# Attention two query tiles a step, tiles at multiples of 512 bytes, first transfers by need, and a spread output border in a fused attention and recurrence layer

## The chip, the cores and the metric

The kernel runs on one core of one Trainium2 chip. The time is device microseconds of one execution of the whole program. TensorE is PE, VectorE is DVE, ScalarE is ACT, GpSimd is POOL and SyncE is SP; PEld is PE's loading of stationary operands.

## The reference

One layer on x, 512 tokens by 2048 features in fp32: normalization, one input projection, an attention group and a recurrence group side by side, one output projection and the residual.

```python
h = rms_norm(x, norm_w)
q, k, v, g_attn, xr, g_lru = split(h @ w_in)     # 1024 | 256 | 256 | 1024 | 1024 | 1024 columns
attn_out = attention_group(q, k, v, ...)          # 8 heads of 128, 2 key/value heads, RMS norm and RoPE on q, k
lru_out = lru_group(xr, ...)                      # 4-tap convolution, then a gated linear scan forward and one backward
mixed = concat([rms_norm(attn_out, attn_norm_w) * silu(g_attn),
                rms_norm(lru_out, lru_norm_w) * silu(g_lru)])
return x + mixed @ w_out                          # w_out is 2048 x 2048
```

## The kernel before, in words

**Products.** Every fp32 operand is split into two tiles, `hi` (rounded, by an ACT cast) and `lo` (the rest, by a DVE subtraction); `wsplit` (L199 to L207) does so for the weights. `mm3` (L145 to L148) issues three matmuls per product: hi·hi, hi·lo, lo·hi. A matmul streams 512 columns of the moving operand past a stationary tile of 128x128, and PE loads the next stationary tile while the present one's columns stream.

**Memory.** Pools are stacked in the on-chip memory from two sides. On the left lie constants, raw weights (`wr`), split weights and the turned x (`xw`), later the outputs stage's residual tiles and part of its operands (`out`). On the right lies first a tile `end` of 24 floats a partition (L100), then the rings of hidden tiles (`hq`), the recurrence (`lru`), keys and values (`qkv`), a second pool of split weights (`wx`, which `wsplit` uses every other time while it is open), attention (`att`) and the final stage (`fin`). So the size of `end` decides at which address, modulo 512 bytes, all tiles on the right begin. PSUM has eight banks: four of tag `pj`, taken by `pj()` mostly for projections, and four of tag `mm`, taken in a ring by `mm()` for scores, transposes and values.

**Start.** `xload` fetches x in chunks of 256 features (the first in two halves), `wraw` fetches raw weights (the first in two halves on ACT's queue), and `columns` (L176 to L182) turns the norm's gain vector `nw_st` on PE, so that x's evacuation can scale by it. `xturn` (L227 to L234) turns x by four PE transposes a tile and evacuates it on ACT and DVE. Until then `busy` issues small warm-up matmuls (L935): WARM of them in front, WARM2 behind the first transposes.

**Stages.** The projection of the recurrence's input (`proj_feat`, L283) runs to about 40 us of the trace, the two halves of the recurrence with the other projection as filler to about 220, K, V and Q to about 285 (`proj_tok`, L321), attention to about 441, the attention's gate projection to 495, and the outputs to 650.

**Attention.** `weave` (L324) alternates a chain and a filler: each `yield n` of `attention` (L608) lets the gates' projections advance by n yields, each six matmuls on a `pj` bank. One step is one query tile of one head: `weights` (L567) makes scores (three matmuls on an `mm` bank), takes the row maximum on DVE (L574), exponentiates on ACT (L577) and scales on POOL (L579); two steps later `turn_weights` (L582) turns the weights by four transposes on an `mm` bank (L586), with a cast on ACT (L588) and a subtraction on DVE (L589); after four tiles `values` (L591) makes the head's output on an `mm` bank and copies it out on DVE (L600). `turned` (L561, through `turn`, L534) turns the queries of a later head by four transposes. Within a step the order is scores, (turned queries), (values), turned weights. The gates' sigmoid products (`gate`, L634 to L645) run on ACT and DVE among these.

**Outputs.** The last product is made from seven block products a level instead of eight, in two passes over P1, Q6, Q5, Q7 and P2, Q3, Q4 (`PASS`, L797). `uses` (L799) lists them in order; `prepare` (L814) splits raw or summed weight blocks into a ring of seven operand tiles, of which entries 0 to 2 lie in `fin` on the right and 3 to 6 in `out` on the left. The left operands, eight mixed tiles made by `seven` (L693), lie on the right for numbers 0 to 4 and in `out` for 5 to 7. The matmuls are L902; `done` (L858) adds each product into the residual tiles on DVE and stores them. `last_gates` (L1095), advanced by `outputs` once at each P1 use, makes the last three left operands. ACT's, DVE's and SP's instructions there stand in the order in which the program writes them.

Of the kernel before, what the change touches and what calls it, by code (L numbers as in the profile page):

```python
# [11 lines left out]
F32 = mybir.dt.float32  # L12
# [5 lines left out]
P = 128  # L18
# [5 lines left out]
NH = 8  # L24
# [16 lines left out]
WARM, WARM2 = 13, 6  # L41


STEPS = 2
# [12 lines left out]
def hybrid_kernel(  # L57
# [42 lines left out]
    opened("end", "right").tile([P, 24], F32, tag="end", name="end")  # L100
# [87 lines left out]
    def wraw(w, r0, c0, nk=1, queue=nc.sync):  # L188

        raw = pools["wr"].tile([P, 2, SEQ], F32, tag="wr", bufs=3, name=nm("wr"))  # L190
        src = w[r0 : r0 + 2 * P, c0 : c0 + SEQ].rearrange("(k p) e -> p k e", p=P)
        for k in range(nk):
# [6 lines left out]
    def wsplit(raw, k):  # L199

        turn_of[0] += k
        pool = pools["wx" if "wx" in pools and turn_of[0] % 2 else "xw"]
        hi = pool.tile([P, SEQ], F32R, tag="wh", bufs=4, name=nm("wh"))
        lo = pool.tile([P, SEQ], F32R, tag="wl", bufs=4, name=nm("wl"))
        nc.scalar.copy(hi, raw[:, k, :])  # L205
        nc.vector.tensor_sub(lo, raw[:, k, :], f(hi))  # L206
        return hi, lo  # L207
# [10 lines left out]
    def xload(c, nk=1):  # L218

        xc = b4(shape=(P, NT, 2 * P))  # L220
        for k in range(nk):
            ks = slice(k * 2 * P // nk, (k + 1) * 2 * P // nk)
            cs = slice(c * 2 * P + ks.start, c * 2 * P + ks.stop)
            nc.sync.dma_start(xc[:, :, ks], xf[:, cs].rearrange("(t p) d -> p t d", p=P))
            yield xc
# [341 lines left out]
    def weights(q, g, t):  # L567

        qh, ql = q
        tt = slice(t * P, (t + 1) * P)  # L570
        sc = mm()
        mm3(sc, qh[:, tt], ql[:, tt], kth[g], ktl[g], True, True)
        mx = pools["att"].tile([P, 1], F32, tag="mx", bufs=6, name=nm("mx"))
        nc.vector.tensor_reduce(mx, sc, axis=AX.X, op=ALU.max, negate=True)  # L574
        p = k2()
        sm = pools["att"].tile([P, 1], F32, tag="sm", bufs=6, name=nm("sm"))
# [31 lines left out]
    def attention(rots):  # L608

        qs, ps_, pts = {h: turned(rots[0], h) for h in range(2)}, {}, {}  # L610
        yield 13
        last = NH * NT
        for i in range(last + 3):
            h, t = divmod(i, NT)
            if i < last:
                ps_[i] = weights(qs[h], h // G, t)
                if t == 0 and h + 2 < NH:
                    qs[h + 2] = turned(rots[(h + 2) // G], (h + 2) % G)
            j = i - 3
            if j >= 0 and j % NT == NT - 1:  # L620
                values(j // NT, *pts.pop(j // NT))
            j = i - 2
            if 0 <= j < last:
                h, t = divmod(j, NT)
                if t == 0:
# [67 lines left out]
    def seven(src, op, hi, lo):  # L693

        src = halves(src)
        res = combine(src, op)
        for to, part in ((slice(0, 3), src[:, 1:4]), (slice(3, 7), res)):
            nc.scalar.copy(hi[:, to], part)
            nc.vector.tensor_sub(lo[:, to], part, f(hi[:, to]))

# [96 lines left out]
    TAIL = 2  # L797
# [43 lines left out]
    def outputs(work):  # L841

        bank, tmp, at = {}, {}, [0]
# [13 lines left out]
        def done(g, name, s):  # L857
# [14 lines left out]
            elif name == "Q7":  # L872
# [3 lines left out]
                v.tensor_add(b10, b10, tmp["c", s])  # L876
# [32 lines left out]
        for n, use in enumerate(order_):  # L909
# [6 lines left out]
            if g == 0 and not second and k == 0:  # L916
                next(work, None)
# [28 lines left out]
    with tc.high_priority():  # L946
        xs, ws = xload(0, 2), wraw(w_in, 0, C_XR, 2, nc.scalar)
        xc, raw = next(xs), next(ws)
        nc.scalar.dma_start(nw_st, norm_w.rearrange("(k p) -> k p", p=P))
# [4 lines left out]
        first = [wsplit(raw, 0)]  # L954
# [103 lines left out]
    def build(i, pair, where):  # L1058
        mixed[i][1] = hi, lo = where(7)
        seven(pair, ALU.subtract, hi, lo)  # L1060

    for q in range(4):
        for _ in range(2):
            next(fill, None)
        build(q, hp[q], lambda n: kept(pools["fin"]))
# [3 lines left out]
    def later():  # L1069
# [6 lines left out]
        build(4, ap_[0], lambda n: [hring.tile([P, n, H], F32R, name=nm(t)) for t in ("mh", "ml")])  # L1076
# [18 lines left out]
    def last_gates():  # L1095
        yield
        build(5, ap_[1], lambda n: last_mixed[0])
        yield
        todo = gate(gs, ap_[2:], R_AN + 4, fin_s)
        for _ in range(3):  # L1100
            next(todo)
        yield
        build(6, ap_[2], lambda n: last_mixed[1])
        drain(todo)
        yield
        build(7, ap_[3], lambda n: last_mixed[2])
        yield
# [48 lines left out]
```

## Time and profile before

| quantity | value |
|---|---|
| median of three runs (lowest, highest) | 658.29 us (656.95, 658.40) |
| the profiled execution's own time | 657.07 us |
| its span, first to last instruction | 655.3 us |
| PE busy | 647.8 us in 2960 instructions |
| DVE, ACT, POOL busy | 485.8, 344.4, 96.5 us |
| granted TensorE clock | full in every slice |
| PE waits in the view of waits | three, of 1.5, 1.1 and 0.5 us |

Views of the profile: the page sums up each engine; the view of waits says for which tile an engine waited, written by whom and at which line; the chain of waits follows the work that ended last back in time; windows and the timeline show a stretch. A row as `L588 ACT CAST pt<-mm` is line 588 on ACT, writing tile `pt` from tile `mm`; what stands in brackets is the idle time before it and what ended it. A matmul's listed duration overlaps its neighbours, so what PE pays is the distance from one start to the next.

### The profile page before, as it was taken

Reading aid. Unit: us, or ns where it says so; the run is one execution under the profiler, and the core shown is the slowest. Engines: PE = TensorE matmul, PEld = TensorE weight load, DVE = VectorE, ACT = ScalarE, POOL = GpSimd, SP = SyncE. Lnnn points to the kernel's source line nnn. Section 1 sums busy time; section 2 is a strip of 40 time slices with the busy share of each in tenths; the row PEclk is TensorE's granted clock in tenths of the full one; section 3 lists DMA queues with packets and bytes.
Section 4 is the critical chain, followed back from the end, with each engine's and each line's share of the span. In section 5 each row is a group of like instructions: output and inputs, shape, how many; then the busy total and the mean of one; then the engine's idle time right before and its main releaser. Section 6 shows DMA issues by size and latency. Waiting matters only on the chain.

```text
span 655.3 us, 8600 instructions
## 1 busy us (share of the span) xinstructions
PE 647.8 (99%) x2960; PEld 532.1 (81%) x2960; DVE 485.8 (74%) x832; ACT 344.4 (53%) x639; POOL 96.5 (15%) x127
## 2 busy tenths in 40 slices
PE   8999999999999999999999999999999999999997
PEld 6888888888888888888888888888888878888875
DVE  5778679977687925855955568439948997698994
ACT  3543799489856515454735456335434564344441
POOL 0000000000022312132543435411000000100000
PEclk9999999999999999999999999999999999999999
DMA  9933253322334331446776678663355667585322
GB/s 292 312 107 113 65 139 95 98 65 65 97 114 129 95 98 33 122 141 147 170 177 149 196 150 193 151 144 111 96 191 197 256 208 248 179 297 177 131 78 96
DMA packets 53067, 96.96 MB, mean 148 GB/s; under 512 B 4316, under 2 KB 14688, under 8 KB 52896
## 3 DMA queue, kind: packets, MB, share of 16 engines
q1 hardware_dynamic: 45648, 75.17, 36.2%
q0 software_dynamic: 7056, 20.72, 13.6%
q10 hardware_dynamic: 320, 0.53, 0.3%
q8 instruction: 23, 0.38, 0.2%
q14 instruction: 20, 0.16, 0.1%
HBM read 92.21 MB, written 20.98 MB: 173 GB/s over the span
## 4 chain that ended last, share of the span: by engine, by line
PE 96%; DVE 1%; DMA 1%; issue 1%; ACT 0%; ACTq 0%; DVEq 0%
PE pj L146 20%; PE pj L148 20%; PE pj L147 20%; PE mm L902 12%; PE pj L902 9%; PE mm L146 3%; PE mm L148 3%; PE mm L147 3%; PE mm L586 2%; PE mm L231 1%; PE pj L292 1%; PE mm L534 1%; DMA nw_st<-in_norm_w_dram 1%; DVE ol L717 0%; DMA rw<-in_w_out_dram 0%
## 5 line engine op out<-in xcount | busy, mean ns | idle before, releaser
L146 PE MATMUL pj<-x,wh 128*128 128x512 f32 x376 | 150.5, 400 | 0.0
L148 PE MATMUL pj<-x,wl 128*128 128x512 f32 x376 | 146.8, 390 | 0.0
L147 PE MATMUL pj<-x,wh 128*128 128x512 f32 x376 | 146.6, 390 | 0.0
L205 ACT CAST wh<-wr 128x512 fp32r<-128x512 f32 x144 | 86.1, 618 | 70.4 <-PE pj L148 26.2
L206 DVE TENSOR_TENSOR wl<-wr,wh 128x512 fp32r<-128x512 f32 x144 | 98.7, 706 | 29.7 <-ACT wh L205 29.7
L148 PEld LDWEIGHTS pj<-x,wl 128*128 128x128 f32 x376 | 70.6, 188 | 15.3
L147 PEld LDWEIGHTS pj<-x,wh 128*128 128x128 f32 x376 | 70.8, 188 | 13.5
L146 PEld LDWEIGHTS pj<-x,wh 128*128 128x128 f32 x376 | 70.7, 188 | 13.5
L146 PE MATMUL pj<-wh,x 128*128 128x512 f32 x192 | 75.3, 392 | 0.0
L148 PE MATMUL pj<-wh,x 128*128 128x512 f32 x192 | 75.2, 392 | 0.0
L147 PE MATMUL pj<-wl,x 128*128 128x512 f32 x192 | 75.1, 391 | 0.0
L716 ACT CAST oh<-rw 128x512 fp32r<-128x512 f32 x94 | 54.8, 619 | 32.6 <-PE mm L902 17.7
L717 DVE TENSOR_TENSOR ol<-rw,oh 128x512 fp32r<-128x512 f32 x94 | 60.6, 686 | 9.7 <-ACT oh L716 6.7
L902 PE MATMUL mm<-ol,mh 128*128 128x512 f32 x128 | 50.3, 393 | 0.5 <-DVE ol L717 0.5
L902 PE MATMUL mm<-oh,mh 128*128 128x512 f32 x128 | 50.2, 392 | 0.0
L902 PE MATMUL mm<-oh,ml 128*128 128x512 f32 x128 | 50.2, 392 | 0.0
L588 ACT CAST pt<-mm 128x512 fp32r<-128x512 f32 x32 | 18.7, 586 | 52.7 <-PE mm L586 52.7
L147 PEld LDWEIGHTS pj<-wl,x 128*128 128x128 f32 x192 | 36.1, 188 | 7.9
L146 PEld LDWEIGHTS pj<-wh,x 128*128 128x128 f32 x192 | 36.0, 188 | 7.9
L148 PEld LDWEIGHTS pj<-wh,x 128*128 128x128 f32 x192 | 36.0, 188 | 7.9
L574 DVE TENSOR_REDUCE mx<-mm 128x1 f32<-128x512 f32 x32 | 22.1, 690 | 23.9 <-PE mm L148 23.4
L902 PE MATMUL pj<-ol,mh 128*128 128x512 f32 x96 | 37.9, 394 | 0.0
(207 smaller groups left out, 1110.2 us busy)
## 6 DMA issues: line engine op xcount, KB each, us to landing
wr<-in_w_in_dram SPq DMA_DIRECT2D x71, 512.0 KB, 3.7
rw<-in_w_out_dram SPq DMA_DIRECT2D x63, 256.0 KB, 3.7
ts<-in_w_out_dram POOLq DMA_DIRECT2D x24, 512.0 KB, 6.5
rw<-ts SPq DMA_DIRECT2D x31, 256.0 KB, 4.9
ts<-ts POOLq DMA_DIRECT2D x8, 512.0 KB, 6.1
xt<-in_x_dram SPq DMA_DIRECT2D x8, 512.0 KB, 8.9
b<-in_x_dram SPq DMA_DIRECT2D x7, 512.0 KB, 8.0
out_dram<-xt POOLq DMA_DIRECT2D x12, 256.0 KB, 3.4
```

Source lines behind the costliest of these rows:

```text
L146: nc.tensor.matmul(acc, lh, rh, start=start, stop=False)
L147: nc.tensor.matmul(acc, lh, rl, start=False, stop=False)
L148: nc.tensor.matmul(acc, ll, rh, start=False, stop=stop)
L205: nc.scalar.copy(hi, raw[:, k, :])
L206: nc.vector.tensor_sub(lo, raw[:, k, :], f(hi))
L231: nc.tensor.transpose(pt[:, t * P : (t + 1) * P], xc[:, t, ks], ident)
L574: nc.vector.tensor_reduce(mx, sc, axis=AX.X, op=ALU.max, negate=True)
L586: nc.tensor.transpose(pt[:, s * P : (s + 1) * P], p[:, s * P : (s + 1) * P], ident)
L588: nc.scalar.copy(pth[:, :, tt], p3)
L716: nc.scalar.copy(hi, src)
L717: nc.vector.tensor_sub(lo, src, f(hi))
L902: nc.tensor.matmul(bank[name, s], lh[:, a, ts_], rh, start=i == 0 and j == 0, stop=i == 7 and j == 2,)
```

## The change

Five things change together.

1. The tile `end` has 120 floats instead of 24, and attention's two sorts of one-column tiles (`mx`, `sm`) have 16 buffers instead of 6. In the built program all tiles on the right begin at 0 mod 512 bytes; before they began at 384, attention's `k` tiles at 192. Those on the left lie at 0 in both.
2. The first transfers are dealt to SP's and ACT's queues anew, the first weight's rounding moves from ACT to DVE, and the warm-up matmuls are 9, 1 and 4 instead of 13 and 6.
3. One step of attention takes two query tiles, in another order, with four filler yields a step instead of two.
4. Two of the additions behind Q7 are held and made in the second pass.
5. `seven` and `build` become generators that stop after each part, and `last_gates` makes the last left operands in 13 pieces spread over the ring's uses 0 to 21, with ACT's Silu and one DVE operation a gate in place of a sigmoid and two.

```diff
-WARM, WARM2 = 13, 6
+WARM, WARM1, WARM2 = 9, 1, 4
...
-STEPS = 2
+STEPS = 4
...
-    opened("end", "right").tile([P, 24], F32, tag="end", name="end")
+    opened("end", "right").tile([P, 120], F32, tag="end", name="end")
...
-    def wraw(w, r0, c0, nk=1, queue=nc.sync):
+    def wraw(w, r0, c0, queues=(nc.sync,)):
...
-    def wsplit(raw, k):
+    def wsplit(raw, k, rounded=nc.scalar.copy):
...
-        nc.scalar.copy(hi, raw[:, k, :])
+        rounded(hi, raw[:, k, :])
...
-    def xload(c, nk=1):
+    def xload(c, queues=(nc.sync,)):
...
-        for i in range(last + 3):
-            h, t = divmod(i, NT)
-            if i < last:
-                ps_[i] = weights(qs[h], h // G, t)
-                if t == 0 and h + 2 < NH:
-                    qs[h + 2] = turned(rots[(h + 2) // G], (h + 2) % G)
-            j = i - 3
-            if j >= 0 and j % NT == NT - 1:
-                values(j // NT, *pts.pop(j // NT))
-            j = i - 2
-            if 0 <= j < last:
...
-                turn_weights(ps_.pop(j), t, *pts[h])
-            yield STEPS
+        for d in range(2 * NH + 3):
+            h, half = divmod(d - 4, 2)
+            if h >= 0 and half == 0:
+                values(h, *pts.pop(h))
+            h, half = divmod(d - 2, 2)
+            if 0 <= h < NH:
...
+                for t in (2 * half, 2 * half + 1):
+                    turn_weights(ps_.pop((h, t)), t, *pts[h])
+            h, half = divmod(d, 2)
+            if h < NH:
+                if half == 1 and h + 2 < NH:
+                    qs[h + 2] = turned(rots[(h + 2) // G], (h + 2) % G)
+                for t in (2 * half, 2 * half + 1):
+                    ps_[h, t] = weights(qs[h], h // G, t)
+            yield STEPS * (d < 2 * NH + 2)
...
-    TAIL = 2
+    TAIL, PIECES, LAST_USE = 2, 13, 22
...
                 v.tensor_sub(b01, b01, bank[name, s])
-                v.tensor_add(b10, b10, tmp["c", s])
+                held.append((b10, tmp["c", s]))
...
-            if g == 0 and not second and k == 0:
+            if second and k and held:
+                b10, c = held.pop(0)
+                nc.vector.tensor_add(b10, b10, c)
+            if n * PIECES // LAST_USE != (n - 1) * PIECES // LAST_USE:
                 next(work, None)
...
-        xs, ws = xload(0, 2), wraw(w_in, 0, C_XR, 2, nc.scalar)
+        queues = nc.sync, nc.scalar
+        xs, ws = xload(0, queues), wraw(w_in, 0, C_XR, queues)
+        nc.scalar.dma_start(nw_st, norm_w.rearrange("(k p) -> k p", p=P))
         xc, raw = next(xs), next(ws)
-        nc.scalar.dma_start(nw_st, norm_w.rearrange("(k p) -> k p", p=P))
         next(xs), next(ws)
...
-        first = [wsplit(raw, 0)]
+        busy(WARM1)
+        first = [wsplit(raw, 0, nc.vector.tensor_copy)]
         xturn(xc, 0)
         busy(WARM2)
...
     def last_gates():
-        yield
-        build(5, ap_[1], lambda n: last_mixed[0])
-        yield
-        todo = gate(gs, ap_[2:], R_AN + 4, fin_s)
-        for _ in range(3):
-            next(todo)
-        yield
-        build(6, ap_[2], lambda n: last_mixed[1])
-        drain(todo)
-        yield
-        build(7, ap_[3], lambda n: last_mixed[2])
-        yield
+        yield from build(5, ap_[1], lambda n: last_mixed[0])
+        for i in (6, 7):
+            for e in range(2):
+                k = 2 * (i - 6) + e
+                sg, dst = fin_s(), ap_[i - 4][:, e, :]
+                nc.scalar.activation(sg, gs[k], AF.Silu)
+                nc.vector.scalar_tensor_tensor(
+                    dst, dst, v1(R_AN + 4 + k), sg, op0=ALU.mult, op1=ALU.mult
+                )
+                yield
+            yield from build(i, ap_[i - 4], lambda n: last_mixed[i - 5])
```

On PE in attention, the step before the one with the first gates, here of the kernel before: `mm_2956` holds scores, `mm_2968` turned queries, `mm_2975` turned weights, `pj` gate projections.

```order
L146 MATMUL mm_2956<-kt_2207,b_540_2654 128x512 [waits DVE_49]
L147 MATMUL mm_2956<-kt_2207,b_540_2654 128x512
L148 MATMUL mm_2956<-kt_2207,b_540_2654 128x512
L534 MATMUL mm_2968<-ident,ev_2420 128x128 [waits DVE_49]
L534 MATMUL mm_2968<-ident,ev_2422 128x128
L534 MATMUL mm_2968<-ident,ev_2424 128x128
L534 MATMUL mm_2968<-ident,ev_2426 128x128
L586 MATMUL mm_2975<-ident,k_587_2871 128x128 [waits DVE_49,Pool_49]
L586 MATMUL mm_2975<-ident,k_587_2871 128x128 x3
L146 MATMUL pj_2522<-x_99_499,wh_2940 128x512
```

The same engine and place in the changed kernel, the step in which the first gates are made: `mm_3029` and `mm_3036` hold turned weights, `mm_3044` turned queries, `mm_3051` and `mm_3062` scores.

```order
L588 MATMUL mm_3029<-ident,k_587_2866 128x128 [waits DVE_49,Pool_49]
L588 MATMUL mm_3029<-ident,k_587_2866 128x128 x3
L588 MATMUL mm_3036<-ident,k_591_2877 128x128 [waits DVE_49,PE_49,Pool_49]
L588 MATMUL mm_3036<-ident,k_591_2877 128x128 x3
L536 MATMUL mm_3044<-ident,ev_2415 128x128 [waits Activation_49]
L146 MATMUL mm_3051<-kt_2202,b_549_2696 128x512 [waits Activation_49]
L147 MATMUL mm_3051<-kt_2202,b_549_2696 128x512
L148 MATMUL mm_3051<-kt_2202,b_549_2696 128x512
L146 MATMUL mm_3062<-kt_2202,b_549_2696 128x512 [waits DVE_49]
L147 MATMUL mm_3062<-kt_2202,b_549_2696 128x512
L148 MATMUL mm_3062<-kt_2202,b_549_2696 128x512
```

Two runs of turned weights now stand first, then the queries, and two scores end the step; the fifth `mm` tile takes the bank of the first and waits for DVE.

On DVE at the same place in the changed kernel: `wl` are low parts of weights, `ev` and `hs` gate products, `pt_2936` the low part of the turned weights, `mx` row maxima.

```order
L207 TENSOR_TENSOR wl_3095<-wr_3092,wh_3094 128x512
L207 TENSOR_TENSOR wl_3099<-wr_3092,wh_3098 128x512
L646 SCALAR_TENSOR_TENSOR ev_2992<-ev_2992,vec,k_625_3021 128x512
L646 SCALAR_TENSOR_TENSOR ev_2994<-ev_2994,vec,k_626_3022 128x512
L647 TENSOR_TENSOR hs_873<-hs_873,ev_2992 128x512
L591 TENSOR_TENSOR pt_2936<-mm_3029,pt_2935 128x4x128
L591 TENSOR_TENSOR pt_2936<-mm_3036,pt_2935 128x4x128
L541 TENSOR_TENSOR b_631_3043<-mm_3044,b_631_3043 128x512
L576 TENSOR_REDUCE mx_3055<-mm_3051 128x1
L576 TENSOR_REDUCE mx_3066<-mm_3062 128x1
```

And in the kernel before, where the first gates are made there.

```order
L574 TENSOR_REDUCE mx_3060<-mm_3056 128x1
L644 SCALAR_TENSOR_TENSOR ev_3019<-ev_3019,vec,k_629_3048 128x512
L644 SCALAR_TENSOR_TENSOR ev_3021<-ev_3021,vec,k_630_3049 128x512
L645 TENSOR_TENSOR hs_878<-hs_878,ev_3019 128x512
L600 COPY av_2889<-mm_3067 128x512
L645 TENSOR_TENSOR hs_878<-hs_878,ev_3021 128x512
L644 SCALAR_TENSOR_TENSOR ev_3023<-ev_3023,vec,k_631_3050 128x512
L578 RECIPROCAL sm_3063<-sm_3063 128x1
```

The gate products stood behind the step's row maximum and beside a values copy; they now stand ahead of the subtraction that frees the first turned weights' bank.

On ACT at the very start, before: the two transfers of `wr_142` are the first weight's halves, `nw_st` is the gain vector.

```order
L194 DMA wr_142<-in_w_in_dram 128x512
L949 DMA nw_st<-in_norm_w_dram 16x128
L194 DMA wr_142<-in_w_in_dram 128x512
L952 ACT_TABLE_LOAD
L952 ACTIVATE table<-ones 128x1
L205 CAST wh_152<-wr_142 128x512
L233 ACTIVATE x_24_161<-mm_156,nw 128x512
```

And in the changed kernel, where `b_18_137` is the second half of x's first chunk.

```order
L956 DMA nw_st<-in_norm_w_dram 16x128
L226 DMA b_18_137<-in_x_dram 128x4x128
L195 DMA wr_139<-in_w_in_dram 128x512
L960 ACT_TABLE_LOAD
L960 ACTIVATE table<-ones 128x1
L235 ACTIVATE x_24_158<-mm_153,nw 128x512
L206 CAST wh_174<-wr_139 128x512
```

The gain vector goes first, half a chunk of x comes to this queue, one weight half goes to SP's queue behind x's first half, and the first cast is gone from ACT.

More of the change, by code (lines that the diff above doesn't have):

```diff
@@ L185, in v1 @@
         return vec[:, r : r + 1]
-    def wraw(w, r0, c0, nk=1, queue=nc.sync):
+    def wraw(w, r0, c0, queues=(nc.sync,)):
         raw = pools["wr"].tile([P, 2, SEQ], F32, tag="wr", bufs=3, name=nm("wr"))
         src = w[r0 : r0 + 2 * P, c0 : c0 + SEQ].rearrange("(k p) e -> p k e", p=P)
-        for k in range(nk):
+        nk = len(queues)
+        for k, queue in enumerate(queues):
             ks = slice(k * 2 // nk, (k + 1) * 2 // nk)
@@ L216, in hybrid_kernel @@
     ssq = const([P, NT, KT // 2], "ssq")
-    def xload(c, nk=1):
+    def xload(c, queues=(nc.sync,)):
         xc = b4(shape=(P, NT, 2 * P))
-        for k in range(nk):
+        nk = len(queues)
+        for k, queue in enumerate(queues):
             ks = slice(k * 2 * P // nk, (k + 1) * 2 * P // nk)
             cs = slice(c * 2 * P + ks.start, c * 2 * P + ks.stop)
-            nc.sync.dma_start(xc[:, :, ks], xf[:, cs].rearrange("(t p) d -> p t d", p=P))
+            queue.dma_start(xc[:, :, ks], xf[:, cs].rearrange("(t p) d -> p t d", p=P))
             yield xc
@@ L611, in attention @@
         yield 13
[L612 to L625 removed]
+        for d in range(2 * NH + 3):
[4 more added lines that the diff above has]
+            if 0 <= h < NH:
+                if half == 0:
                     pts[h] = [
@@ L699, in seven @@
             nc.vector.tensor_sub(lo[:, to], part, f(hi[:, to]))
+            yield
     def kept(pool, n=7):
@@ L841, in outputs @@
     def outputs(work):
-        bank, tmp, at = {}, {}, [0]
+        bank, tmp, at, held = {}, {}, [0], []
         def take(key):
@@ L1059, in build @@
         mixed[i][1] = hi, lo = where(7)
-        seven(pair, ALU.subtract, hi, lo)
+        return seven(pair, ALU.subtract, hi, lo)
     for q in range(4):
@@ L1075, in later @@
             yield next(todo)
-        build(4, ap_[0], lambda n: [hring.tile([P, n, H], F32R, name=nm(t)) for t in ("mh", "ml")])
+        drain(
+            build(4, ap_[0], lambda n: [hring.tile([P, n, H], F32R, name=nm(t)) for t in ("mh", "ml")])
+        )
         yield from todo
```

8 lines of the change are left out of this document (5 added, 3 removed).

## Prediction

> **What bounds the kernel now.** The page comes first: its span, the engines' busy time and the granted clock by slices.
>
> ```profile
> span 655.3 us, 8600 instructions
> PE 647.8 (99%) x2960; PEld 532.1 (81%) x2960; DVE 485.8 (74%) x832; ACT 344.4 (53%) x639; POOL 96.5 (15%) x127
> PEclk9999999999999999999999999999999999999999
> ```
>
> PE works through 99% of the span at the full clock, so time can come only from what PE waits for and from how fast its instructions follow one another. PE's part of the view of waits comes second.
>
> ```profile
> PE mm L180 <- DMA nw_st<-in_norm_w_dram: 1.5, 1, 1.5
> PE mm L935 <- POOL ones L154: 1.1, 1, 1.1
> PE mm L902 <- DVE ol L717: 0.5, 1, 0.5
> ```
>
> That is 3.1 us in three waits; the second stands before the first instruction and is not touched. The larger reserve is the pitch. The chain of waits gives it for the outputs stage, where all is PE: start, duration, matmuls of 512 columns.
>
> ```profile
> 495.19 2.72 PE mm L902 x12
> 497.92 2.75 PE pj L902 x12
> 500.67 2.80 PE mm L902 x12
> 503.47 2.77 PE pj L902 x12
> 506.24 2.72 PE mm L902 x12
> 508.96 2.79 PE pj L902 x12
> 522.84 2.77 PE mm L902 x12
> 525.61 2.97 PE pj L902 x12
> ```
>
> Each row holds two uses of the operand ring. The built program says where their operands lie: left operands in this stretch on the right-hand side of the on-chip memory at 384 mod 512 bytes, ring entries 0 to 2 there too, entries 3 to 6 on the left at 0 mod 512. The first and fifth rows use entries 0,1 and 1,2 (both operands at 384): 2.72. The third and sixth use 4,5 and 3,4 (one operand at 384, one at 0): 2.80 and 2.79. Rows with one use of each kind lie between, and two from step 20 on, where the left operand itself lies on the left, are turned about. So where both operands agree a matmul takes 2.72/12 = 226.7 ns, and 6.7 ns more, (2.80 − 2.72)/12, where they differ. The same shows between two projection stages, in the table of windows (columns: window, length, PE, its weight loads, DVE, ACT, POOL, clock, DMA share, GB/s).
>
> ```profile
> 140.00:158.00 18.00, 18.00 (x81) 14.88 (x80) 11.85 (x15) 17.92 (x27) 0.00 (x0) 1.00 0.21 60
> 239.00:257.00 18.00, 18.00 (x79) 14.53 (x78) 6.62 (x7) 5.50 (x17) 1.32 (x4) 1.00 0.17 51
> ```
>
> In the first window all operands lie at 0; in the second every other weight tile comes from the right-hand pool at 384. Nothing waits in either, yet 18 us hold 81 matmuls and 79.
>
> **The change part by part.** *The tile of 120 floats* moves every right-hand tile from 384 (attention's `k`: 192) to 0 mod 512, so both operands of every 512-wide matmul agree. Outputs: of 672 matmuls I count 348 that stream past a next stationary tile of another address: 348 × 6.7 ns = 2.3 us. K, V and Q: two matmuls in 18 us are 0.45 us, over 48 us 1.2 us. Attention: 96 score matmuls (keys at 384, queries at 0) and the borders of other stages, at most some 200 × 6.7 = 1.3, at least 0; I take 0.7. Sum −4.2 us (−2.9 to −4.8: were the mixed rows only noise, the outputs would give half).
>
> The Trainium skill, page "TensorE: Matmul & The Clock Gate", Part 2 (step-by-step, step 1), says that the array reads the streaming and the stationary operand through two independent ports, so that a weight load takes nothing from the running matmul. By that rule this term would be 0; the rows 2.72 and 2.80 speak against it.
>
> *Two query tiles a step.* Score matmuls and transposes stay as many; two runs of four transposes become one of eight. Four rows of the timeline (transposes, and the second matmul behind them) price that.
>
> ```profile
> 287.63 0.60 PE L586 MATMUL mm<-ident,k 128*128 128x128 f32 x4
> 288.30 0.40 PE L147 MATMUL pj<-x,wh 128*128 128x512 f32 x1
> 291.53 0.60 PE L534 MATMUL mm<-ident,ev 128*128 128x128 f32 x4
> 292.64 0.40 PE L147 MATMUL pj<-x,wh 128*128 128x512 f32 x1
> ```
>
> Behind a run of four the second matmul starts 0.67 us after the run, behind eight (L534's and L586's) 1.11. Two runs of four with a matmul of 0.23 saved between them are 2 × 0.67 − 0.23 = 1.11: no gain but in the few slower pitches behind a run's end. I take 30 ns for each of 16 runs that end is saved, −0.5 us (0 to −0.75).
>
> The price is in the PSUM ring. Tag `mm` has four banks, and an odd step now takes five in a row: two for turned weights, one for turned queries, two for scores. So the second score matmul waits until the first turned weights have been read, by ACT's cast and DVE's subtraction. One such chain in the trace:
>
> ```profile
> 305.68 0.40 PE L146 MATMUL mm<-kt,b 128*128 128x512 f32 x1
> 306.38 0.60 PE L586 MATMUL mm<-ident,k 128*128 128x128 f32 x4
> 307.01 0.59 ACT L588 CAST pt<-mm 128x512 fp32r<-128x512 f32 x1 [2.75 <-PE mm L586]
> 307.63 0.69 DVE L589 TENSOR_TENSOR pt<-mm,pt 128x512 fp32r<-128x512 f32 x1 [0.36 <-ACT pt L588]
> ```
>
> From the run's start to the end of the subtraction: 307.63 + 0.69 − 306.38 = 1.94 us. PE arrives after three runs (twelve transposes at about 0.11, from 1.11 − 0.67 for four) and three score matmuls: 3 × 0.44 + 3 × 0.23 = 2.0. Slack 0, before anything that stands ahead on ACT or DVE. In even steps the values product stands ahead and its copy on DVE is waited for; there I find some 0.65. So 0.1 for ordinary odd steps, 0.2 in sum (0 to 1). In step 5 the first gates stand ahead.
>
> ```profile
> 317.53 1.28 ACT L640 ACT_TABLE_LOAD   x1
> 318.82 2.20 ACT L640 ACTIVATE k<-ev 128x512 f32<-128x512 f32 x4
> 319.49 2.26 DVE L644 SCALAR_TENSOR_TENSOR ev<-ev,vec,k 128x512 f32<-128x512 f32 x2
> ```
>
> Counted from the table load, the sigmoids end at 1.28 + 2.20 = 3.5, then cast 0.59 and subtraction 0.69: 4.8. PE, six fill matmuls and the 2.0 later, is there at 6 × 0.23 + 2.0 = 3.4. The wait is 1.3 us (0, if the fill's tail covers it, to 2.5, if the two weight casts of 0.6 go first). Queued behind it on PE is everything. Sum for attention's waits +1.5 (0 to +3.5).
>
> *First transfers by need.* The start of the trace:
>
> ```profile
> 1.13 2.96 PE L935 MATMUL mm<-ones 128*128 128x256 bf16 x13 [1.13 <-POOL ones L154]
> 4.46 0.62 ACT L205 CAST wh<-wr 128x512 fp32r<-128x512 f32 x1 [0.83 <-DMA wr<-in_w_in_dram]
> 5.55 0.20 PE L180 MATMUL mm<-ident,nw_st 16*128 16x16 f32 x1 [1.46 <-DMA nw_st<-in_norm_w_dram]
> 5.68 0.66 PE L231 MATMUL mm<-ident,b 128*128 128x128 f32 x4
> 6.38 0.69 ACT L233 ACTIVATE x<-mm,nw 128x512 fp32r<-128x512 f32 x1 [1.30 <-PE mm L231]
> 7.12 1.20 PE L292 MATMUL pj<-x,wh 128*128 128x512 f32 x4
> ```
>
> The small gain vector, issued behind a weight half, lands last and holds the transposes of x to 5.68; the weight half, first on its queue, had landed by 4.46. Now the gain vector goes first on ACT's queue, and the weight half is second on SP's, behind x. It then lands 0.5 to 0.9 later, 5.0 to 5.4 (estimate: half a transfer more in front), and its cast, 0.62, moved to DVE, ends by 6.0. The first half of x, first on SP's queue as before, can be turned from about 4.6; transposes and ACT's pass of 0.69 end at 6.0 to 6.2. The first product starts near 6.2 instead of 7.12: −0.9 (−0.3 to −1.3). Behind it PE waits for nothing in the stage (no further row in the view of waits), so the gain carries as far as the later transfers keep ahead; the low end allows for one that doesn't.
>
> *Left operands and border of the outputs.* Two additions are held back until the second pass.
>
> ```profile
> 621.64 0.69 DVE L876 TENSOR_TENSOR xt<-xt,ev 128x512 f32<-128x512 f32 x1
> 623.44 0.69 DVE L876 TENSOR_TENSOR xt<-xt,ev 128x512 f32<-128x512 f32 x1
> 624.04 0.69 DVE L717 TENSOR_TENSOR ol<-tc,oh 128x512 fp32r<-128x512 f32 x1
> 624.78 0.50 PE L902 MATMUL mm<-ol,mh 128*128 128x512 f32 x1 [0.54 <-DVE ol L717]
> ```
>
> The operand ends at 624.73 behind both additions. Without the second it ends by 624.04, and the matmul would have been due at 624.78 − 0.54 = 624.24: the wait of 0.54 goes, and the row's neighbours show no other DVE result that PE waits for. The row of 2.97 at 525.61 against 2.77 gives 0.2 more, since spreading and the single Silu take four DVE operations of 0.69 out of that stretch. −0.9 (−0.4 to −1.0). The last left operand is now made at use 21 of the ring, 21 × 1.38 = 29 us in, and wanted at use 24, four us on; if cast and subtraction came late, up to +0.8. The pieces and fills between attention and outputs lie under 48 us of gate projection: 0.
>
> The sum: −4.2 − 0.5 + 1.5 − 0.9 − 0.9 = −5.0 us. The profiled execution took 657.07, 1.2 below the median of the three runs; half-way is 657.7, and 657.7 − 5.0 = 652.7. With the parts' bounds, 650 to 655.
>
> **The rivals.** *The address isn't it.* The operands that agree also lie on the same side of the memory, and the change leaves sides as they are. For it: the scores, both on the right but at 384 and 0, take (306.38 − 305.68)/3 = 233 ns, which a row of two decimals hardly tells from 227; that they are slow speaks for the address, faintly. Then −5.0 + 4.2 = −0.8: 656.9.
>
> *Slower: the PSUM ring waits in every two-tile step.* If DVE, three quarters busy, reaches the first subtraction late in all 11 steps where five tiles meet four banks, as step 5 does, each costs 1.3: 14.3 instead of 1.5, so −5.0 + 12.8 = +7.8: 665.5. It decides from 0.6 us of delay a step (6.5/11). Against: DVE waits for ACT in the row of 307.63, so it is mostly early.
>
> *The clock opens later.* Four warm-ups fewer in front (228 ns each by 2.96/13) and a gap of like length behind them. Were the clock at half speed 2 to 3 us longer, a few matmuls would double: +0.8 to +2.5, 653.5 to 655.2. Against: the granted clock is 1 from the first slice. The page named above, Part 1, gives a window of 3.4 us that runs by itself and judges PE's activity; no row here shows its phase.
>
> *No wait in attention.* Then −6.5: 651.2. For it: the chain of 1.94 fits into 2.0, and step 5 has a bound of 0.
>
> **How the numbers follow.** Forecast 0.58, later clock 0.12, no attention wait 0.14, address not it 0.10, slower 0.06. The range leaves out the last two and thin tails: 649.6 to 656.2. About 0.3%, 2 us, is what a measurement of this kernel tells from no change. Faster by more: 0.58 + 0.14 + most of 0.12, 0.82; within: 0.11; slower: 0.07.
>
> **What would show it.** Twelve matmuls of the outputs in 2.72 throughout; 81 instructions in a window of the Q projection; the first product near 6.2; no wait of PE on L717's like; a wait of PE's scores on DVE in step 5 and nearly none elsewhere. Output rows that stay at 2.80 would prove the forecast's largest term wrong; waits at many score matmuls, the second.

## The result, and the profile after

The changed kernel takes 652.56 us (median of five runs, 651.78 to 653.15), the kernel before, beside it, 658.40 (five runs, 656.95 to 659.00). The ratio is 0.9912, with a 95% interval of 0.9898 to 0.9927: faster by 0.9%, against a forecast of 652.7. The profiled execution took 652.63 with a span of 650.9. That of before (657.07, 655.3) was one of its quicker ones, so the two traces differ by 4.4 us and the medians by 5.8.

The page of the changed kernel, the lines shown of before:

```profile
span 650.9 us, 8579 instructions
PE 643.4 (99%) x2955; PEld 532.2 (82%) x2955; DVE 479.6 (74%) x829; ACT 348.4 (54%) x639; POOL 95.4 (15%) x127
PEclk9999999999999999999999999999999999999999
```

PE still fills 99% of the span; the difference in its busy time, 647.8 − 643.4 = 4.4 us, is the whole difference in span. PE's part of the view of waits:

```profile
PE mm L146 <- DVE pt L591: 1.1, 1, 1.1
PE mm L942 <- POOL ones L154: 1.1, 1, 1.1
PE mm L146 <- DVE av L602: 0.9, 1, 0.9
```

The waits for the gain vector and for the outputs' operand are gone. Two new ones stand in attention, both at a score matmul (L146 on an `mm` tile): one for the low part of turned weights, as forecast, and one for the copy of the values, which was not. The chain of waits in the outputs:

```profile
494.36 2.72 PE mm L906 x12
497.08 2.72 PE pj L906 x12
...
521.56 2.72 PE mm L906 x12
```

Every dozen takes 2.72, also those that took 2.79 and 2.80.

To see where the time went, the same matmul is looked up in both traces. Counted are the matmuls of 512 columns that write a `pj` tile, 2016 in each kernel and in the same order but for attention's pairing; the times are their starts in us. (The forecast's window from 239 to 257 us is no measure in the changed kernel: the work has moved, and the window holds other instructions, eight short transposes among them.)

| matmul | stage that it ends | before | after | shift | change in the stage |
|---|---|---|---|---|---|
| 31st | start | 15.40 | 14.26 | −1.14 | −1.14 |
| 960th | recurrence, K, V, Q | 256.92 | 254.27 | −2.65 | −1.51 |
| 1561st | attention, part of the gate projection | 456.94 | 456.12 | −0.82 | +1.83 |
| 2016th | rest of the projection, outputs | 645.25 | 640.85 | −4.40 | −3.58 |

Three stages won 6.2 us and attention gave back 1.8. Behind the last matmul nothing changed.

The start, in the chain of waits of the changed kernel:

```profile
1.12 2.10 PE mm L942 x9
3.24 0.26 PE mm L180
...
3.82 0.90 PE mm L233 x4
...
5.50 1.19 PE pj L294 x4
```

The gain vector is there at 3.2 instead of 5.5, the first half of x by 3.6 (the timeline has its first transpose at 3.62), and the first product starts at 5.50 instead of 7.12. Of these 1.6 us a part is given back a little later, in the timeline:

```profile
10.64 0.42 DVE L242 SCALAR_TENSOR_TENSOR b<-b 128x256 f32<-128x256 f32 x1
10.98 1.29 DVE L207 TENSOR_TENSOR wl<-wr,wh 128x512 fp32r<-128x512 f32 x2
12.19 1.41 DVE L236 SCALAR_TENSOR_TENSOR x<-mm,nw,x 128x512 fp32r<-128x512 f32 x2
12.69 0.39 PE L146 MATMUL pj<-x,wh 128*128 128x512 f32 x1
12.99 0.50 PE L147 MATMUL pj<-x,wh 128*128 128x512 f32 x1
13.33 0.39 PE L148 MATMUL pj<-x,wl 128*128 128x512 f32 x1
```

From 12.69 the starts lie 0.30 and 0.34 apart instead of 0.23: PE follows DVE, which evacuates x (L236) behind the squares and the weights' low parts. Some 0.2 us are lost here; a like amount had been lost at 8.9, where PE followed ACT's evacuation of the tile before.

Attention, the step with the first gates, where `pt` is the turned weights and `hs`, `ev` the gate products:

```profile
312.96 1.29 DVE L207 TENSOR_TENSOR wl<-wr,wh 128x512 fp32r<-128x512 f32 x2
313.30 1.67 ACT L642 ACTIVATE k<-ev 128x512 f32<-128x512 f32 x3
314.16 1.41 DVE L646 SCALAR_TENSOR_TENSOR ev<-ev,vec,k 128x512 f32<-128x512 f32 x2
314.87 1.04 ACT L590 CAST pt<-mm 128x512 fp32r<-128x512 f32 x2
315.49 0.69 DVE L647 TENSOR_TENSOR hs<-hs,ev 128x512 f32<-128x512 f32 x1
316.09 1.28 DVE L591 TENSOR_TENSOR pt<-mm,pt 128x512 fp32r<-128x512 f32 x2
316.83 0.50 PE L146 MATMUL mm<-kt,b 128*128 128x512 f32 x1 [1.14 <-DVE pt L591]
```

The score matmul was due at 315.52 (0.23 behind the last, at 315.29) and starts at 316.83: 1.3 us, the forecast's number. ACT's first cast ends at about 315.4, behind the sigmoids, and DVE makes a gate product (315.49) before it turns to the subtraction.

The step with the second gates:

```profile
388.06 1.79 POOL L608 TENSOR_TENSOR asum<-asum,k 128x512 f32<-128x512 f32 x1
388.96 3.29 DVE L207 TENSOR_TENSOR wl<-wr,wh 128x512 fp32r<-128x512 f32 x2
389.35 2.36 POOL L581 TENSOR_SCALAR k<-k,sm 128x512 f32<-128x512 f32 x2
...
401.25 0.69 DVE L647 TENSOR_TENSOR hs<-hs,ev 128x512 f32<-128x512 f32 x1
401.86 0.68 DVE L602 COPY av<-mm 128x512 f32<-128x512 f32 x1
402.60 0.50 PE L146 MATMUL mm<-kt,b 128*128 128x512 f32 x1 [0.94 <-DVE av L602]
```

Here two subtractions of weights took DVE 3.29 us, while POOL worked beside them (in the step of the first gates two took 1.29). The gate products came late, and the values were copied behind them: 402.60 − 401.27 − 0.23 = 1.1 us lost, where the forecast saw slack.

### The profile page after: what moved, and what is told of

Read it like the earlier page. It is cut to its first block, busy times and chain, and to the rows that moved or that the text cites. A ratio compares the mean times of both kernels' runs of the same rounds, so it can differ in the third digit from the quotient of the medians.

```text
span 650.9 us, 8579 instructions
## 1 busy us (share of the span) xinstructions
PE 643.4 (99%) x2955; PEld 532.2 (82%) x2955; DVE 479.6 (74%) x829; ACT 348.4 (54%) x639; POOL 95.4 (15%) x127
## 4 chain that ended last, share of the span: by engine, by line
PE 96%; DVE 3%; issue 0%; DVEq 0%; POOL 0%; POOLq 0%
PE pj L146 19%; PE pj L148 19%; PE pj L147 19%; PE mm L906 13%; PE pj L906 10%; PE mm L146 3%; PE mm L148 3%; PE mm L147 3%; PE mm L588 2%; PE mm L233 1%; DVE wl L207 1%; PE pj L294 1%; PE mm L536 1%; DVE ev L646 1%; PE mm L942 0%; DVE hs L647 0%
## 5 line engine op out<-in xcount | busy, mean ns | idle before, releaser
L146 PE MATMUL pj<-x,wh 128*128 128x512 f32 x376 | 147.6, 393 | 0.0
L146 PEld LDWEIGHTS pj<-x,wh 128*128 128x128 f32 x376 | 70.6, 188 | 14.5
L720 ACT CAST oh<-rw 128x512 fp32r<-128x512 f32 x94 | 56.2, 620 | 36.4 <-PE mm L906 15.8
L146 PE MATMUL pj<-wh,x 128*128 128x512 f32 x192 | 75.0, 391 | 0.0
L721 DVE TENSOR_TENSOR ol<-rw,oh 128x512 fp32r<-128x512 f32 x94 | 61.7, 688 | 10.3 <-ACT oh L720 8.9
L146 PEld LDWEIGHTS pj<-wh,x 128*128 128x128 f32 x192 | 36.1, 188 | 7.6
L906 PE MATMUL pj<-oh,ml 128*128 128x512 f32 x96 | 37.4, 389 | 0.0
L906 PE MATMUL pj<-oh,mh 128*128 128x512 f32 x96 | 37.4, 389 | 0.0
```

The costliest lines, as they stand in the source:

```text
L146: nc.tensor.matmul(acc, lh, rh, start=start, stop=False)
L720: nc.scalar.copy(hi, src)
L721: nc.vector.tensor_sub(lo, src, f(hi))
L906: nc.tensor.matmul(bank[name, s], lh[:, a, ts_], rh, start=i == 0 and j == 0, stop=i == 7 and j == 2,)
```

## Experiments

The stretches named are those of the table above: the attention stretch is from the 960th to the 1561st such matmul (before 200.02 us, after 201.85), the outputs stretch from the 1561st to the 2016th (before 188.31, after 184.73). Each run was timed beside the kernel before, whose medians were 658.16 to 658.58.

**The addresses alone.** The kernel before with

```diff
-    opened("end", "right").tile([P, 24], F32, tag="end", name="end")
+    opened("end", "right").tile([P, 120], F32, tag="end", name="end")
...
-        mx = pools["att"].tile([P, 1], F32, tag="mx", bufs=6, name=nm("mx"))
+        mx = pools["att"].tile([P, 1], F32, tag="mx", bufs=16, name=nm("mx"))
```

and the same for `sm`.

> The kernel before with the border tile of 120 floats and 16 one-column buffers, nothing else: all tiles on the right at 0 mod 512. If the address decides the pitch, all rows of twelve output matmuls take 2.72, the window 239 to 257 holds 81 or more matmuls, and the time falls by about 5.1 us against the kernel before (2.7 in the outputs, 1.3 in K, V and Q, 1.1 in attention, as the two traces differ): some 653.3. If the sides of the memory decide, the rows stay at 2.79 to 2.80 and the time within 0.5 us of before.

Measured: 655.41, ratio 0.9960 (0.9946 to 0.9973): 2.7 us faster, half of what I had expected. The window that held 79 matmuls now holds 81, in the table of windows:

```profile
239.00:257.00 18.00, 18.00 (x81) 14.93 (x80) 6.62 (x7) 5.25 (x15) 1.62 (x4) 1.00 0.21 66
```

So the address does set the pitch, with nothing else changed. Where the rest went: the attention stretch is 200.06, not a bit shorter, so the 1.1 us that I had read out of the two traces for attention was wrong. And the outputs' waits grew:

```profile
PE mm L902 <- DVE ol L717: 0.8, 1, 0.8
PE pj L902 <- DVE ol L717: 0.4, 1, 0.4
```

A faster PE meets the same late DVE: 1.2 us of waits instead of 0.5. The outputs stretch is 186.55, 1.8 shorter instead of 2.6. The profiled execution also lost 1.7 us at the start:

```profile
5.53 1.04 PE mm L231 x4
...
7.85 1.71 PE pj L292 x4
```

Four products took 1.71 us where those of before took 1.20: PE ran there at 0.43 us a matmul. The trace's record of the granted clock shows full clock from 10.31 us on in this execution, and from 4.37 in that of before.

**Right-hand tiles at 256 and at 64 mod 512.** The changed kernel with

```diff
-    opened("end", "right").tile([P, 120], F32, tag="end", name="end")
+    opened("end", "right").tile([P, 56], F32, tag="end", name="end")
```

and, in a second kernel, with 104.

> The changed kernel with a border tile of 56 floats: all right-hand tiles at 256 mod 512, the left ones at 0. If only equal addresses mod 512 are fast, 5.1 us come back: 657.7, and mixed rows of twelve output matmuls take 2.80. If 256 is enough, the time stays at 652.6 and the rows at 2.72.

> The changed kernel with a border tile of 104 floats: right-hand tiles at 64 mod 512. If any difference mod 512 costs the same, 657.7 with mixed rows of 2.80, as at 384. If the cost grows with the distance or needs one past a quarter, the rows lie between 2.72 and 2.80 and the time between 652.6 and 657.7.

Measured at 256: 652.16, ratio 0.9913 (0.9897 to 0.9929), as the changed kernel; at 64: 657.02, ratio 0.9987 (0.9976 to 0.9997), nearly all given back. The chain in the outputs at 256, and then at 64:

```profile
495.11 2.72 PE mm L906 x12
```

```profile
503.64 2.80 PE mm L906 x12
...
509.22 2.72 PE mm L906 x12
```

At 64 the row at 509.22 is one with both operands on the right, both at 64: equal addresses are fast there too.

What counts is the address modulo 256: 0 and 256 agree, 64 and (before) 384, which is 128 mod 256, don't. The multiples of 512 in the change are more than is needed. The outputs stretch says it by itself: 184.73 at 256, 187.25 at 64. Sides of the memory are the same in all three kernels, so that rival fell.

The Trainium skill, page "TensorE: Matmul & The Clock Gate", Part 2 (step-by-step, step 1), has two independent read ports, by which a weight load takes nothing from the running matmul. The pitches here don't fit it: 226.7 ns a matmul (2.72/12) where the two addresses agree mod 256, 233 (2.80/12) where they don't. That the weight load is what slows the matmul is argued from this; no run takes the load away.

**One query tile a step.** The changed kernel with the attention loop of before and `STEPS = 2`.

> The changed kernel with the attention loop of before (one query tile a step, two filler yields). If attention's loss of 1.8 us comes from the two PSUM ring waits of 1.3 and 1.1 us, PE has no wait there and the time falls by about 2.4 us, to 650.2. If it comes from elsewhere (runs of eight, scores behind transposes, a collision that both loops have), the time stays near 652.6 or rises by the 0.5 us of 16 more run ends.

Measured: 651.63, ratio 0.9907 (0.9891 to 0.9924), 0.9 under the changed kernel in medians. In the traces the attention stretch falls from 201.85 to 200.06, by 1.8 us, and PE's view of waits has no row of attention:

```profile
PE mm L942 <- POOL ones L154: 1.1, 1, 1.1
PE pj L294 <- ACT x L235: 0.3, 1, 0.3
```

The two waits cost 1.3 + 1.1 = 2.4 us, so about 0.6 of them was paid back: that is what the runs of eight transposes were worth. So the first theory held, and the new attention loop, in the order that the change gives it, is a loss.

**Filler between the runs and the scores.** The changed kernel with each step's four yields split:

```diff
                 for t in (2 * half, 2 * half + 1):
                     turn_weights(ps_.pop((h, t)), t, *pts[h])
+            yield STEPS // 2 * (d < 2 * NH + 2)
             h, half = divmod(d, 2)
...
-            yield STEPS * (d < 2 * NH + 2)
+            yield STEPS // 2 * (d < 2 * NH + 2)
```

> The changed kernel with each step's four filler yields split: two behind the turned weights, two behind the scores. Runs of eight stay; the ring waits get two yields of slack, 12 x 0.227 = 2.7 us. If the ring is the cause, the waits of 1.3 and 1.1 go, and the time falls by about 2.4 us to 650.2. If the gates' work on DVE stops PE in any order, a wait stays at another tile and the time falls by less than 1 us.

Measured: 650.70, ratio 0.9887 (0.9872 to 0.9902): the best of all, 1.9 under the changed kernel. The runs of eight are kept and the ring has slack. PE's view of waits has one row of attention left:

```profile
PE mm L146 <- DVE pt L591: 0.3, 1, 0.3
```

The attention stretch is 199.59, 0.5 under that with one tile a step and 2.3 under the changed kernel's. One wait, at the first gates, stays with 0.3 (by the starts of the matmuls 0.5).

**Three yields and one.** The same with `yield 3` behind the turned weights and `yield 1` behind the scores.

> The changed kernel with three filler yields behind the turned weights and one behind the scores. The ring's slack grows from 2.7 to 4.1 us, so the last wait of PE in the version with two and two (0.5 us with the first gates) goes as well: 650.2 against its 650.7. If the slack is taken from the next step's transposes instead (one yield between scores and the turned weights), PE waits there for POOL or ACT and the time is above 650.7.

Measured: 657.67, ratio 0.9989 (0.9978 to 1.0000). The first expectation missed, and of the second only the direction came true: it is 7 us worse than with two and two, but PE does not wait at the transposes. The waits are of the old kind, only larger:

```profile
PE mm L146 <- DVE pt L591: 5.3, 2, 3.0
```

In the trace the first gates' four sigmoids and the weights' casts now stand ahead of the first turned weights' cast on ACT, and two gate products, two sums and two weight subtractions ahead of the subtraction on DVE. The two gate products took 2.94 us there, with POOL's scaling beside them, against 1.41 in the changed kernel. ACT's and DVE's order in attention isn't written out but follows from when things are issued, and another split brought the gates to a worse place. The timeline behind the first wait shows a second loss, and the page's row of the granted clock has it too:

```profile
322.74 0.77 PE L146 MATMUL mm<-kt,b 128*128 128x512 f32 x1 [3.03 <-DVE pt L591]
323.31 0.63 PE L147 MATMUL mm<-kt,b 128*128 128x512 f32 x1
323.73 0.63 PE L148 MATMUL mm<-kt,b 128*128 128x512 f32 x1
...
325.79 0.40 PE L147 MATMUL pj<-x,wh 128*128 128x512 f32 x1
```

```profile
PEclk9999999999999999999899998999999999999999
```

After three idle microseconds matmuls follow each other at 0.43 us (323.31 to 323.73) for some 3 us, and then at 0.23 again. By the trace's record of the granted clock it fell to half from 322.27 to 325.68, and once more from 404.19 to 407.60, behind the other wait, of 2.3 us: the two dips of the row.

**The gates' products on POOL.** The changed kernel with

```diff
+            if sig is k2:
+                nc.gpsimd.tensor_scalar(g, g, v1(row + e), 0.0, op0=ALU.mult, op1=ALU.add)
+                nc.gpsimd.tensor_mul(g, g, s)
+                nc.gpsimd.tensor_mul(dst, dst, g)
+                continue
             nc.vector.scalar_tensor_tensor(g, g, v1(row + e), s, op0=ALU.mult, op1=ALU.mult)
```

> The changed kernel with the gates' products in attention on POOL (three operations for DVE's two, same values). If DVE's queue, two products of 0.7 and one of 0.6 ahead of the subtraction, makes the wait of 1.3 us in the step of the first gates, it falls to about 0.5, what ACT's sigmoids ahead of the cast leave, and the second gates' wait goes: some 651. If ACT alone makes it, both waits stay and the time is 652.6; if POOL now comes late with the scaled weights, PE waits at the transposes for POOL, and the time is above 652.6.

Measured: 651.55, ratio 0.9896 (0.9883 to 0.9909), 1.0 under the changed kernel. What stays in attention is the wait that ACT leaves:

```profile
PE mm L146 <- DVE pt L591: 0.5, 1, 0.5
```

By the starts it is 316.61 − 315.69 − 0.23 = 0.7 us instead of 1.3: of the first wait 0.6 us are DVE's queue and 0.7 ACT's. The second is gone too, as the expectation had it. Two runs below lack it without this edit; but there DVE's two weight subtractions were quick, and here they took 4.05 us, longer than in the changed kernel. The attention stretch is 200.43.

**The start alone.** The kernel before with the change's edits to `wraw`, `wsplit`, `xload`, the first block and the warm-up counts.

> The kernel before with the new first transfers, the first cast on DVE and the new warm-ups, nothing else. By the trace of the changed kernel the first product starts at 5.5 instead of 7.1, 0.45 of it is lost to DVE at 13 us, and 1.2 us are carried to the end: 657.2. If the gain at the start is eaten later by transfers that both kernels share, the time is that of before, 658.4.

Measured: 656.52, ratio 0.9983 (0.9974 to 0.9991): 1.6 us in medians, 1.1 by the ratio, with 0.6 to 1.7 in its interval; the expected 1.2 lies in it. Its profiled execution carried only 0.1, since the first weight's halves landed at 5.6 and 8.8 there (4.7 and 7.7 in the changed kernel), with a wait at the first product:

```profile
PE pj L294 <- DVE wh L206: 0.6, 1, 0.6
```

With the weight half second on its queue the first product hangs on how fast transfers run in that execution.

**The first cast on ACT.** The changed kernel with

```diff
-        first = [wsplit(raw, 0, nc.vector.tensor_copy)]
+        first = [wsplit(raw, 0)]
```

> The changed kernel with the first weight's cast on ACT, as before the change. ACT then casts from 4.75 to 5.4 and evacuates x only after it, to 6.1, so the first product starts at about 6.1 instead of 5.5. If the stage behind is paced by PE, 0.6 us are lost: 653.2. If it is paced by DVE and the transfers, as the 0.45 us given back at 13 us say, less than 0.3 is.

Measured: 652.83, ratio 0.9924 (0.9908 to 0.9939). The first product starts at 6.16, and the 31st matmul at 14.46 against 14.26: of 0.66 us at the first product 0.2 is left 8 us later. The stage is not paced by its first product. The second gate wait of attention is absent in this execution (stretch 200.75).

**The squares later.** The changed kernel with the squares of x's first chunk on DVE behind the second chunk's evacuation:

```diff
             xturn(xc, 1)
-            xsquare(xc, 0)
...
+        if (c, e) == (0, 3):
+            xsquare(xc, 0)
```

> The changed kernel with DVE's four squares of x's first chunk behind the second chunk's evacuation. If DVE's order there is what gives back 0.45 us of the start, the pitches of 0.30 and 0.34 at 12.7 and 13.0 us fall to 0.23 and some 0.2 to 0.45 us are won: 652.2. If the transfers set the pace, PE waits at the same place for the weights and nothing is won.

Measured: 652.81, ratio 0.9916 (0.9901 to 0.9931): no gain, and the 31st matmul at 14.44. The pitches behind 12.7 us did fall to 0.23, so the squares had made them. But in this execution the weight's second half landed at 8.05 instead of 7.66, PE lost 0.37 instead of 0.23 us around 9 us behind ACT's evacuation of x, and the first product came 0.16 later: what was won there was lost to other terms.

Oddly this kernel, whose attention is that of the changed one, shows no second gate wait at all (its stretch is 200.73), like that with the first cast on ACT; the kernel at 256 showed 1.5, that without warm-up 1.1 and that at 64 0.5 in the view of waits, the changed one 0.9. The traces tell what differs. The two weight subtractions at that place took 3.83 us (at 256), 3.44 (no warm-up), 3.29 (changed) and 2.95 (at 64), and 2.14 and 1.86 in the two without the wait. The waits stand in the same order and differ by nearly the same amounts. The weights were not late: each cast had ended before the subtraction that reads it began. In each of these traces the pair ended some 0.54 us behind POOL's last scaling of attention weights. In the changed kernel's trace none of the 419 such DVE operations (two tensors in, 128x512) that ran without POOL's arithmetic beside them took over 0.70 us; the first of this pair took 2.28. So the wait hangs on when POOL makes its scalings. Why POOL comes up to 2 us later in some executions isn't shown.

**No warm-up.** The changed kernel with

```diff
-WARM, WARM1, WARM2 = 9, 1, 4
+WARM, WARM1, WARM2 = 1, 0, 0
```

> The changed kernel with one warm-up matmul in front and none later. If PE's speed at the start hangs on work done before, the transposes of x and the first products run at half speed longer than in the changed kernel (0.90 for four transposes there, 0.43 instead of 0.23 a matmul) and 1 to 2.5 us are lost: some 654. If not, the time stays at 652.6 and the first products at 0.23 to 0.30.

Measured: 653.39, ratio 0.9931 (0.9915 to 0.9947), 0.8 slower than the changed kernel. The first product starts at the same time, but at half the speed:

```profile
5.55 2.08 PE pj L294 x4
7.63 0.85 PE mm L233 x4
```

The 31st matmul comes at 15.97, 1.7 later than in the changed kernel. But the execution of the kernel at 64, with all warm-ups, had the same rows (2.00 and 0.85), while the one at 256 did not. So warm-ups don't make full speed at 5.5 us certain; that they make it likelier is argued from the 0.8 us and one trace.

**The outputs alone.** The kernel before with the held additions and the 13 pieces.

> The kernel before with the held additions and the 13 pieces of the last left operands, nothing else. The waits of 0.7 at 624 us and 0.2 at 526 us go: 0.9 us, 657.5, and PE's view of waits has no row of the output matmuls. The rival: the additions and pieces only move, and delay another operand: 658.4 or more, with a wait at another place in the second pass.

Measured: 657.30, ratio 0.9991 (0.9980 to 1.0002), 0.9 in medians but not clear of nothing by itself. The trace is: the outputs stretch is 187.29 instead of 188.31, 1.0 us less, and no wait at an output matmul is left.

## Why the prediction was right, and where it was not

The time was forecast to 0.2 us and lay in the range. The nearness owes something to errors that cancelled: −5.0 was forecast from a base of 657.7, and the medians differ by 5.8 from 658.40; the two traces differ by 4.4.

- **The addresses**, forecast −4.2: between the traces −1.5 (recurrence, K, V, Q) and, after the 1.0 that the outputs edit wins alone, −2.6 in the outputs: −4.1. The cause is shown by the kernels at 256 and 64. The 0.7 for attention was misplaced: with the addresses alone scores and values won 0.4 us by their pitches there, but the filler's products lost 0.5, and the stretch was as long as before. Alone the edit was worth less, since it raised the outputs' waits; together with the held additions it gave all.
- **Runs of eight**, forecast −0.5 (0 to −0.75): −0.6, by the loops with one and two tiles. With the filler split, the stretch is 0.5 shorter than with one tile in spite of a loss of 0.5, which makes 1.0; how much of that is the order and not the runs, no run parts.
- **The first gates' wait**, forecast 1.3: 1.3, at the forecast place, but its size is partly luck. Counted from the table load (310.44), PE was due at 5.1 us and could go on at 6.4; the forecast had 3.4 and 4.8. It put the whole wait on ACT's sigmoids and cast and had no term for DVE's gate product ahead of the subtraction. The kernel with products on POOL shows ACT's share as 0.7 and DVE's as 0.6.
- **The step that failed:** "in even steps the values product stands ahead and its copy on DVE is waited for; there I find some 0.65". With the second gates the copy stood behind DVE's gate products, and these behind weight subtractions that POOL's scalings stretched: 1.1 us that no term held, here; in two other executions of that order nothing. So attention's waits were 2.4 instead of 1.5, inside their bounds. The slower rival, a wait in all 11 steps, did not happen.
- **The start**, forecast −0.9: −1.1 in the trace, 1.6 alone in medians. The first product came at 5.5, not 6.2, since x's half landed a microsecond sooner than I had taken (it was turned from 3.62, not 4.6); but the stage behind did not carry all of it, against "the gain carries as far as the later transfers keep ahead": ACT's and DVE's evacuation of x was late next.
- **The outputs' border**, forecast −0.9: −1.0.
- **The later clock** was a rival that exists but is not the change's. "The granted clock is 1 from the first slice" was misread, as was the table of before: the page shows a stretch without any record as full. The traces' records begin, with the full clock, at 4.37 us (before) and 5.23 (after); warm-ups of 256 columns lie 0.21 us apart ahead of that and 0.11 behind. Where the record begins later, the first products run at half speed: between their first and eleventh counted matmul, 2.86 us in both traces of the main pair, four executions lost 0.6 to 1.9 us (records from 6.82, 7.21, 9.87 and 10.31), one of them (the addresses alone) with the old start, and that without warm-up 2.1 (10.18). The execution at 64 that lost 1.9 took 658.97, as much above its kernel's median. That this is why other kernels' runs lie 2 us apart, and why the medians differ by more than these traces, is argued, not shown.

The best version keeps the changed kernel and puts half of each step's filler between turned weights and scores: 650.70. What stays open is why the filler in attention lost what the scores won by the addresses, why POOL's scalings come at other times in other executions, and what sets the time at which the full clock begins.

## What to carry to other kernels

Where PE is the bound, read the pitch of like matmuls in the chain of waits, not only its waits: a few nanoseconds on thousands of matmuls were worth more here than every wait together. When work is grouped into longer runs, count the buffers of the ring that the run passes through, and put independent work between the run and the instruction that needs its first buffer back. And price a new wait in the step with the most other work on the freeing engine, not in an ordinary one, and look at what POOL does beside DVE there.

## What the runs showed of the hardware

- A 512-column matmul takes 226.7 ns when the tile that it streams and the stationary tiles have the same address mod 256 bytes, and about 233 when not (differences of 64 and 128 mod 256 alike; the rows of twelve, 2.72 and 2.80 us). Whether the matmul's own stationary tile counts or the next, loaded beside it, these runs don't part.
- In the kernel with three yields and one, waits of 3.0 and 2.3 us were each followed by 3.41 us of half the granted clock, in which a matmul took 0.43 us; single waits of 1.1 us (changed kernel) and 1.5 us (at 256) were not. At the start the full clock began between 4.1 and 10.3 us, with the old and the new warm-ups alike.
- A DVE operation of 128x512 with two tensors in took 0.67 to 0.70 us in the changed kernel's trace without POOL's arithmetic beside it; beside it most took as long, but some more, up to 2.28.

The Trainium skill's page "TensorE: Matmul & The Clock Gate", Part 1, tells of such a half rate after an idle window of about 3.4 us, in windows that run by themselves, with 427 ns for 512 columns. The 0.43 us agree, and so do the two stretches of 3.41 us; waits of 3.0 and 2.3 us, shorter than that window, were enough here.
